# An encoder block at norm2: two steps of the third w_up tile, and splits of the first tile's weights, made earlier

## The chip, the cores and the metric

The kernel runs on one NeuronCore of a Trainium2 chip. A core has five engines that run side by side, each with an instruction stream of its own: TensorE (PE in the profile, its weight loads PEld), VectorE (DVE), ScalarE (ACT), GpSimd (POOL) and SyncE (SP), which here only issues DMAs. They wait for each other by semaphores. The metric is the device time of one execution in microseconds (us).

## The reference

One layer of an encoder on a sequence of 1024 positions with 1024 channels, all in float32. After the token mixers the part that matters here is:

```python
x = x + gate1 * (merged @ w_out[i])                       # the out stage
h2 = rmsnorm(x, g_ffn[i]) * (1 + scale2) + shift2          # norm2
u = depthwise_conv_seq(h2 @ w_up[i], conv_w[i], conv_b[i])  # the up stage
u_val, u_gate = jnp.split(u, 2, axis=-1)
x = x + gate2 * ((jax.nn.gelu(u_gate, approximate=True) * u_val) @ w_down[i])
```

`w_up` has 1024 rows and 5632 columns. The residual `x` is needed for all channels before `rmsnorm` has its scale, so norm2 is a point at which one large product ends and the next can't yet start in full.

## The kernel before, in words

**Precision.** Each float32 operand of a product is split into a high part, rounded to TensorE's fast float32 format, and a low part, the rest. A product is then three matmuls: high by high, high weights by low data, low weights by high data. `split` (L57 and L61) and `operand` (L1135, L1136) make the parts: ScalarE copies the high part, GpSimd or VectorE subtracts to get the low part. One matmul multiplies a 128x128 weight block with 512 columns of data.

**The out stage.** `out_tile(hf, m, ...)` makes one 128-channel tile m of `merged @ w_out` for one half hf of the positions: 24 matmuls (L84 to L86), an update of x on VectorE (L1321), a store of x (L1322), a square for the norm on ScalarE (L1327) and a copy of x scaled by the norm's weights (L1328). The weights of the next tile are loaded (L65) and split (whi by ScalarE, wlo by GpSimd) two buffers ahead. The first half hf = 0 is done for all eight m, then its norm (the sums, a broadcast of the scale by four transposes on PE, L111, and VectorE's multiplication L1352) and its operands B11 and B21 (L1309 on ScalarE, L1310 on VectorE), while PE works on hf = 1.

**The up stage.** The product `h2 @ w_up` is done in 22 tiles, each with two weight tiles (value and gate), by a scheme of Strassen's kind with seven products in place of eight. With `STEPS`, the steps of a tile are named by their weights: "11" and "12" (the weights themselves; their data are B11 and B21, which come from the first half hf = 0 alone), and S2, S1, S3, S4 and "22", whose data T2, T1, T3, B22 and T4 need the second half, and so norm2. Each step is 12 matmuls (L1189 to L1191). The profile's tile names follow: whi and wlo are the parts of "11" and "12", wsh and wsl those of S2 and S1 or of S3 and "22", big those of S4, and x holds B22 and T4 among others.

**A tile's weights.** `a_operands` is a generator with four parts, each run by a `next`: the sums S1, S2 and S3 on GpSimd (L1153 to L1155) and the split of "11" and "12"; the split of S2 and S1 and S4's sum on VectorE (L1162); the split of S3 and "22"; the split of S4. `up_load` fetches a tile's raw weights in two DMAs of 512 KB (L1337), one of value and one of gate rows, into `big` buffers or into `wraw`, of which there are two.

**Around norm2.** Tile 0 is loaded in the out stage, and its sums are made there. Its splits come behind the out stage, as do tile 1's first two parts; the buffers for wsh and wsl (three each) lie in the pool `up`, whose memory is the one that the merged operands held until the last tile of the out stage. `products` makes the steps of a tile as a generator; before the change it yields -1 once within each step, and `advance` runs it to the end of a step. From the last out tile on, PE's order is the written one (`late_mm`): the sums of norm2's squares (L98) with the two halves of tile 0's step "11" between them, the broadcast (L111), tile 1's "11", then "12" of tile 0 and tile 1, and, once T2 is there, the S2 steps of both. VectorE computes, in an order written out by hand (`manual_schedule`), the scaling with the broadcast scale (L1449), T2 (L1452, L1310), T1 (L1458, L1136), T3, B22 and T4; GpSimd makes T4's low parts.

**Order elsewhere.** Outside such hand-written stretches a planner chooses the order of each engine's stream ahead of time, from its own model of durations; a stream is then executed in that order. Tiles of one name in one pool are handed out in the order in which the program asks for them, from the buffers that are free. So a load waits for the tile asked for before it as well as for a free buffer. The loop over t then runs the rest of each tile's steps and, between them, the parts of the next tile's `a_operands`.

Of the kernel before, what the change touches and what calls it, by code (L numbers as in the profile page):

```python
# [19 lines left out]
KT = 8  # L20
FF = 22
# [8 lines left out]
def hybrid_encoder(tc, xT, c, w_ada, small, w_in, p1_bias, p23_bias, na_bias, ln2_mult, ident, w_br, w_out,  # L30
# [1111 lines left out]
    def a_operands(raw, n, work, st, lo_eng=pool, last=False):  # L1142


        a11, a12, a21, a22 = raw[0][:, 0], raw[0][:, 1], raw[1][:, 0], raw[1][:, 1]
        ws = big([128, 2, n, 128])
# [9 lines left out]
        hi, lo = (wpool.tile([128, KT, 128], FR, name=t).rearrange("p (a b) m -> p a b m", a=2)[:, :, :n]  # L1156
                  for t in ("whi", "wlo"))
        pair(raw[0], ("11", "12"), hi, lo, lo_eng)
        yield
        hi, lo = (work(t).tile([128, 2, n, 128], FR, name=t, bufs=3) for t in ("wsh", "wsl"))  # L1160
        pair(ws, ("S2", "S1"), hi, lo)
        dve.tensor_tensor(a12, a12, S2, OP.subtract)  # L1162
        yield
        hi, lo = (work(t).tile([128, 2, n, 128], FR, name=t, bufs=3) for t in ("wsh", "wsl"))
        pair(raw[1], ("S3", "22"), hi, lo)
        yield
        s4 = work("wsl").tile([128, 2, n, 128], FR, name="wsl", bufs=3) if last else big([128, 2, n, 128], FR)
        pair(raw[0][:, 1:2], ("S4",), s4[:, 0:1], s4[:, 1:2])
        yield

    def products(st, n, moving, done, seq=range(7), in_psum=False):

        p, c = {}, {}

        def bank(x_):
            p[x_] = ps.tile([128, 512], FT, name="pj", bufs=6)
            return p[x_]

        def tmp(x_):
            c[x_] = wide()  # L1180
            return c[x_]
        for j in seq:
            a, b = STEPS[j]
            x_ = "abcdacd"[j]
            psum = bank(x_) if j < 4 else p[x_]
            whi, wlo = st[a]
            for k in range(n):
                bhi, blo = moving(b, k)
                pe.matmul(psum, whi[:, k], bhi, start=j < 4 and k == 0, stop=False, skip_group_check=True)  # L1189
                pe.matmul(psum, whi[:, k], blo, start=False, stop=False, skip_group_check=True)  # L1190
                pe.matmul(psum, wlo[:, k], bhi, start=False, stop=k == n - 1, skip_group_check=True)  # L1191
# [163 lines left out]

    m2 = []
    sqa = wide()
    for m in range(KT - 1):
# [6 lines left out]
    sts = [{} for _ in range(FF)]  # L1365
# [8 lines left out]
    late = {n: [] for n in ("B22", "T4")}  # L1374

    with tc.tile_pool(name="up", bufs=2, reuse_waits="tile") as work:
        def conv_in(y, t, hf, src):
            act.activation(y[:, halves[hf]], src, AF.Identity, bias=conv[:, 3, t:t + 1], scale=conv[:, 1, t:t + 1])  # L1378

# [12 lines left out]
        def up_products(t, st, seq=range(7)):  # L1392
            u, ys = [{}, {}], {i: big([128, S]) for i in range(2) if t == FF - 1}

            def done(i, hf, src):
                u[i][hf] = src
                if len(u[i]) == 1 and t < 2:
                    return
                with tc.high_priority(offset=-300 if t == FF - 1 else 0):
                    finish(i, hf)  # L1400

            def finish(i, hf):
                if i not in ys:
                    ys[i] = big([128, S])
                for n in range(2) if t < 2 else (hf,):
                    conv_in(ys[i], t + FF * i, n, u[i][n])
                if len(u[i]) == 2:
                    conv_taps(ys[i], t + FF * i, u[i])
                if len(u[0]) + len(u[1]) == 4:
# [1 line left out]
                    dve.tensor_tensor(ys[0], ys[0], ys[1], OP.mult)  # L1411
                    sp.dma_start(a_scr[t], ys[0])
            return products(st, 4, lambda n, k: late[n][k] if n in late else (ops[n][0][:, k], ops[n][1][:, k]), done,
                            seq)

        raw[1] = up_load(1)
        prep = [a_operands(raw.pop(t), 4, lambda t: work, sts[t], dve) for t in range(2)]
        next(prep[0])
        next(prep[1])
        for _ in range(3):  # L1420
            next(prep[0])
        next(prep[1])
        gens = [up_products(t, sts[t], (0, 4, 1, 2, 3, 5, 6)) for t in range(2)]

        def advance(g):
            for j in g:
# [19 lines left out]
        with tc.manual_schedule(engines={act.engine, dve.engine, pool.engine}):  # L1446
# [45 lines left out]
            for k in range(4):  # L1492
                dve.tensor_tensor(m1[4 + k], m1[4 + k], t2[k], OP.subtract)
                late["T4"].append((half_tile(FR), half_tile(FR)))
                operand(m1[4 + k], *late["T4"][k], pool)
        for g in gens:
            advance(g)
        late_mm.close()
        for t in range(FF):
# [1 line left out]
            if t + 2 < FF:  # L1501
                raw[t + 2] = up_load(t + 2)
            if 0 < t < FF - 1:
                nxt = a_operands(raw.pop(t + 1), 4, lambda t: work, sts[t + 1], last=t + 2 == FF)
                next(nxt)
            elif t == 0:
                nxt = prep[1]
            for j in gens[t] if t < 2 else up_products(t, sts[t]):
# [7 lines left out]
                if t == FF - 1 and j == 3:  # L1516
# [3 lines left out]
                            + [("T3h", 2048, G), ("T3l", 2048, G)])  # L1520
                    for _ in range(3):
                        next(more)
    for p in oppools[::-1]:
        p.release()

# [9 lines left out]
        reserve(work1[n], [(n + e, 2048, G) for e in "hl"])  # L1535
    ends = {}
    sts = [{} for _ in jobs]
    first = a_operands(down_load(*jobs[0]), G, work1.get, sts[0])
# [7 lines left out]
    for n, (g0, q) in enumerate(jobs):  # L1546
        nxt = iter(())
        if n + 1 < len(jobs):
            nxt = a_operands(down_load(*jobs[n + 1]), G, work1.get, sts[n + 1])
        if n < 3:  # L1550
            x3_load(n + 1)
        if n == 2:
# [173 lines left out]
```

## Time and profile before

| | |
|---|---|
| median of three runs (lowest to highest) | 1537.97 us (1537.17 to 1539.8) |
| the profiled execution, its span | 1539.41 us, 1537.3 us |
| PE busy | 1499.0 us, 98% of the span |
| DVE, ACT, POOL busy | 996.0, 770.4, 775.8 us |
| mean granted clock of PE | 0.988 of full speed |
| second half of the out stage | about 816 to 857 us from the span's start |
| norm2's sums, broadcast | 856.17 to 862.98 us |
| first S2 step (T2) | 873.23 us |

The span runs from the first to the last instruction of one execution. In a table of stretches each row has the stretch, its length, the busy time of the engine with the number of its records, the granted clock of PE, the busy share of the DMA engines and what they moved in GB/s. A line of waits has who waited for whom, the total in us, how often and the longest. A line of the chain has start, length and what ran, followed back from the last instruction to what released it. A line of the order of time has start, length, engine, source line, operation, tiles written and read, and in brackets the idle time before it and what ended it; several like operations are merged, their number behind the x.

### The profile page before, as it was taken

How to read it: one execution, taken by the hardware profiler on the slowest of the kernel's cores; microseconds unless marked ns; L12 is line 12 of the kernel's file. 1: busy time of each engine (PE TensorE's matmuls, PEld its weight loads, DVE VectorE, ACT ScalarE, POOL GpSimd, SP SyncE). 2: the span in 40 equal slices, each digit the busy share in tenths (PEclk: the TensorE clock that was granted, in tenths of full speed). 3: DMA queues.
4: the chain of work that ended last, by engine and by line, in shares of the span. 5: the costliest groups of instructions: out<-in, count | busy, mean ns of one | idle time of the engine just before them, and what ended most of it. 6: DMA issues, size and time to landing. Idle time of an engine off the chain costs nothing. (4 is left out here: it accounts for less than half of the span.)

```text
span 1537.3 us, 21792 instructions
## 1 busy us (share of the span) xinstructions
PE 1499.0 (98%) x7740; PEld 1270.1 (83%) x7740; DVE 996.0 (65%) x1892; ACT 770.4 (50%) x1437; POOL 775.8 (50%) x640
## 2 busy tenths in 40 slices
PE   8999999999999999999999899999999998999997
PEld 7988888889798998878888677888888887878787
DVE  6675357575656655645525888876666667786765
ACT  4331566666656566643345454444444447475542
POOL 1021344443335444512267668776777765779721
PEclk8999999999999999999999999999999999999999
DMA  9567333333625456577644112222222224523323
GB/s 352 187 240 258 94 106 81 108 91 104 185 82 153 127 140 171 154 241 232 213 141 154 62 62 96 90 82 83 82 82 85 87 79 162 193 75 124 117 55 110
DMA packets 112436, 205.24 MB, mean 134 GB/s; under 512 B 40484, under 2 KB 53156, under 8 KB 112292
## 3 DMA queue, kind: packets, MB, share of 16 engines
q1 hardware_dynamic: 112056, 203.59, 41.1%
q8 instruction: 61, 1.00, 0.3%
q14 instruction: 47, 0.39, 0.1%
q10 hardware_dynamic: 272, 0.26, 0.1%
HBM read 158.73 MB, written 42.47 MB: 131 GB/s over the span
## 5 line engine op out<-in xcount | busy, mean ns | idle before, releaser
L61 POOL TENSOR_TENSOR wlo<-wraw,whi 128x512 fp32r<-128x512 f32 (+1 forms) x96 | 118.3, 1253 | 172.9 <-ACT whi L57 139.1
L84 PE MATMUL pj<-h,whi 128*128 128x512 f32 x448 | 187.7, 419 | 1.8 <-ACT h L207 1.4
L85 PE MATMUL pj<-h,whi 128*128 128x512 f32 x448 | 177.8, 397 | 1.6 <-DVE h L209 1.6
L86 PE MATMUL pj<-h,wlo 128*128 128x512 f32 x448 | 177.2, 396 | 0.0
L61 POOL TENSOR_TENSOR wsl<-big,wsh 128x512 fp32r<-128x512 f32 (+1 forms) x90 | 123.6, 1395 | 47.7 <-ACT wsh L57 47.7
L639 POOL TENSOR_TENSOR wlo<-wraw,whi 128x512 fp32r<-128x512 f32 x58 | 74.9, 1301 | 117.2 <-ACT whi L638 117.2
L589 DVE TENSOR_TENSOR tl<-T,th 128x512 fp32r<-128x512 f32 (+3 forms) x120 | 77.1, 653 | 72.9 <-ACT th L588 71.4
L1384 DVE SCALAR_TENSOR_TENSOR big<-wc,sm,big 128x256 f32<-128x256 f32 (+1 forms) x132 | 106.9, 859 | 16.1 <-ACT big L1378 15.9
L581 ACT ACTIVATE P<-P,st 128x256 f32<-128x256 f32 x128 | 64.1, 502 | 95.9 <-DVE st L580 95.9
L86 PEld LDWEIGHTS pj<-h,wlo 128*128 128x128 f32 x448 | 85.0, 190 | 18.9
L84 PEld LDWEIGHTS pj<-h,whi 128*128 128x128 f32 x448 | 85.6, 191 | 13.6 <-ACT h L207 1.9
L85 PEld LDWEIGHTS pj<-h,whi 128*128 128x128 f32 x448 | 85.6, 191 | 13.2 <-DVE h L209 3.0
L57 ACT ACTIVATE whi<-wraw 128x1024 fp32r<-128x1024 f32 (+2 forms) x52 | 50.7, 975 | 73.0 <-PE pj L85 27.6
L1384 DVE SCALAR_TENSOR_TENSOR big<-pj,sm,big 128x512 f32<-128x512 f32 x132 | 67.0, 563 | 17.6 <-ACT big L1378 17.6
L61 POOL TENSOR_TENSOR wsl<-wraw,wsh 128x384 fp32r<-128x384 f32 (+1 forms) x46 | 54.4, 1204 | 44.6 <-ACT wsh L57 44.4
L910 POOL TENSOR_SCALAR P<-P,stb 128x288 f32<-128x288 f32 (+1 forms) x32 | 40.2, 1257 | 72.1 <-DVE stb L907 64.7
L588 ACT ACTIVATE th<-T 128x512 fp32r<-128x512 f32 (+3 forms) x120 | 65.6, 566 | 20.3 <-PE T L919 14.0
L1378 ACT ACTIVATE big<-wc,sm 128x512 f32<-128x512 f32 x44 | 35.8, 815 | 69.3 <-DVE wc L1202 42.3
L57 ACT ACTIVATE wsh<-big 128x1024 fp32r<-128x1024 f32 (+1 forms) x45 | 44.7, 998 | 46.2 <-POOL big L1154 32.6
L547 POOL TENSOR_TENSOR vv<-vv 128x512 fp32r<-128x512 f32 (+1 forms) x40 | 42.0, 1069 | 48.5 <-ACT vv L546 48.5
L1410 ACT ACTIVATE big<-big 128x1024 f32<-128x1024 f32 x22 | 23.3, 1060 | 80.0 <-DVE big L1384 80.0
L580 DVE CUSTOM_DVE_ANT_0 P<-S,bias 128x256 f32<-128x256 f32 x128 | 48.9, 419 | 21.3 <-PE S L692 17.1
(395 smaller groups left out, 4799.3 us busy)
## 6 DMA issues: line engine op xcount, KB each, us to landing
wraw<-w_in SPq DMA_DIRECT2D x34, 512.0 KB, 4.2
wada<-w_ada SPq DMA_DIRECT2D x31, 512.0 KB, 7.9
big<-w_up SPq DMA_DIRECT2D x22, 512.0 KB, 5.4
wraw<-w_up SPq DMA_DIRECT2D x22, 512.0 KB, 3.7
as<-big SPq DMA_DIRECT2D x22, 512.0 KB, 3.0
big<-as SPq DMA_DIRECT2D x22, 512.0 KB, 8.0
wraw<-w_down SPq DMA_DIRECT2D x24, 384.0 KB, 3.8
gs<-gs SPq DMA_DIRECT2D x32, 256.0 KB, 2.9
```

The lines of the kernel that those rows point to most:

```text
L57: act.activation(hi, raw, AF.Copy)
L61: lo_eng.tensor_tensor(lo[:, i:i + step], raw[:, i:i + step], f(hi)[:, i:i + step], OP.subtract)
L84: pe.matmul(psum, whi[:, k0 + k], mhi, start=k == 0, stop=False)
L85: pe.matmul(psum, whi[:, k0 + k], mlo, start=False, stop=False)
L86: pe.matmul(psum, wlo[:, k0 + k], mhi, start=False, stop=k == n - 1)
L547: pool.tensor_tensor(lo[:m, cs_], f(lo[:m, cs_]), f(vv[:m, cs_, 0:64]), OP.subtract)
L580: dve.tensor_tensor_reduce(pp, d, bias, -1.0, BIG, OP.add, OP.min, mi)
L581: act.activation(pp, pp, AF.Exp, bias=mi, scale=-1.0, accum_out=li)
L588: act.activation(th[:m, :n], pt[:m, :n], AF.Copy)
L589: dve.tensor_tensor(tl[:m, :n], pt[:m, :n], f(th)[:m, :n], OP.subtract)
L639: pool.tensor_tensor(lo[:, i:i + n], raw[:, i:i + n], f(hi)[:, i:i + n], OP.subtract)
L1384: dve.scalar_tensor_tensor(y[:, dst], src, wt, y[:, dst], OP.mult, OP.add)
```

## The change

Four things are done differently, all around norm2.

- Tile 0's weights are loaded at the start of the second half of the out stage, and its sums, the splits of S2 and S1 and of S3 and "22" are asked for after tiles m = 1, 2 and 4 of it. A new pool `up1` gives them buffers of their own (two for wsh, two for wsl) while the out stage still runs; a third wsh and wsl stays in `up`. Tile 0's split of "11" and "12" and S4's come behind tile m = 6, as the fourth part (`w_at=3`).
- The "11" and "12" rows of tile 2's value weights are loaded once more on their own after m = 5 (two DMAs of 256 KB into `half_tile` buffers) and split there, low parts on GpSimd. Tile 2's later `a_operands` then leaves that split out (`w_at=None`).
- `products` yields -1 after each of its first three groups of three matmuls. Nine matmuls of tile 1's step "11" stand ahead of the broadcast; behind it come the last three, tile 2's "11" and then "12" of tiles 0, 1 and 2. Tile 2's two early results are kept in two new buffers `held`, by one more copy on ScalarE, so that its PSUM bank is freed.
- Tiles 1 and 2 take their sums and S4 parts from new buffers `xb` in place of `big`, and tile 2's convolution, like that of tiles 0 and 1, starts when both halves of a result are there.

The core of the diff:

```diff
+    def a_operands(raw, n, work, st, lo_eng=pool, last=False, w_at=0, spot=None):
+        spot = spot or big
...
+        def outer(at):
+            if w_at == at:
+                hi, lo = (wpool.tile([128, KT, 128], FR, name=t).rearrange("p (a b) m -> p a b m", a=2)[:, :, :n]
+                          for t in ("whi", "wlo"))
+                pair(raw[0], ("11", "12"), hi, lo, lo_eng)
+
+        def s_tiles():
+            pools = [work(t) for t in ("wsh", "wsl")]
+            return [p.tile([128, 2, n, 128], FR, name=t, bufs=b) for (p, b), t in zip(pools, ("wsh", "wsl"))]
+        outer(0)
         yield
+        pair(ws, ("S2", "S1"), *s_tiles())
+        if w_at != 3:
+            dve.tensor_tensor(a12, a12, S2, OP.subtract)
         yield
+        pair(raw[1], ("S3", "22"), *s_tiles())
         yield
+        outer(3)
+        if w_at == 3:
+            dve.tensor_tensor(a12, a12, S2, OP.subtract)
...
-                if k == 1:
+                if k < n - 1:
                     yield -1
...
+            elif j == 4 and hold:
+                act.activation(hold[1], psum, AF.Copy)
+                done(0, 0, hold[1])
...
+    up1 = tc.alloc_tile_pool(name="up1", bufs=2, reuse_waits="tile")
+    reserve(up1, (("wsh", 4096, 2), ("wsl", 4096, 2), ("held", 2048, 2)))
+    s_homes = {n: itertools.cycle([(up1, 2)] * 2 + [None]) for n in ("wsh", "wsl")}
...
+    raw = {0: up_load(0)}
+    prep = [a_operands(raw.pop(0), 4, s_home, sts[0], dve, w_at=3)]
+    held = [up1.tile([128, 512], FT, name="held", bufs=2) for _ in range(2)]
     for m in range(KT - 1):
         m2.append(half_tile())
         out_tile(1, m, sqa, m2[m])
-        if m == 3:
-            raw = {0: up_load(0)}
+        if m in (1, 2, 4):
+            next(prep[0])
+        if m == 5:
+            ahead2 = [half_tile().rearrange("p (b m) -> p b m", b=4) for _ in range(2)]
+            for a, r in enumerate(ahead2):
+                sp.dma_start(r, w_up[2][:, 4 * a:4 * a + 4])
         if m > 3:
             pool.tensor_tensor(m2[m - 4], m2[m], m2[m - 4], OP.subtract)
+    next(prep[0])
+    for n, r in zip(("11", "12"), ahead2):
+        sts[2][n] = [half_tile(FR).rearrange("p (b m) -> p b m", b=4) for _ in range(2)]
+        split(r, *sts[2][n], pool)
...
         add_sums(pcol, sqa, True, False)
         next(gens[0])
+        next(gens[0])
         add_sums(pcol, sq, False, True)
         advance(gens[0])
+        for _ in range(3):
+            next(gens[1])
         bc = bcast(rstd_of(pcol, 4), ps, "pbc")
         advance(gens[1])
-        advance(gens[0])
-        advance(gens[1])
+        advance(gens[2])
+        for g in gens:
+            advance(g)
...
-        for g in gens:
+        for g in gens[:2]:
             advance(g)
```

More of the change, by code (lines that the diff above doesn't have):

```diff
@@ L1140, in hybrid_encoder @@
     names = tuple(b for _, b in STEPS)
-    def a_operands(raw, n, work, st, lo_eng=pool, last=False):
+    def a_operands(raw, n, work, st, lo_eng=pool, last=False, w_at=0, spot=None):
+        spot = spot or big
         a11, a12, a21, a22 = raw[0][:, 0], raw[0][:, 1], raw[1][:, 0], raw[1][:, 1]
-        ws = big([128, 2, n, 128])
+        ws = spot([128, 2, n, 128])
         S2, S1 = ws[:, 0], ws[:, 1]
@@ L1155, in a_operands, with products @@
         pool.tensor_tensor(a21, a11, a21, OP.subtract)
-        hi, lo = (wpool.tile([128, KT, 128], FR, name=t).rearrange("p (a b) m -> p a b m", a=2)[:, :, :n]
-                  for t in ("whi", "wlo"))
-        pair(raw[0], ("11", "12"), hi, lo, lo_eng)
+        def outer(at):
[7 more added lines that the diff above has]
+        outer(0)
         yield
-        hi, lo = (work(t).tile([128, 2, n, 128], FR, name=t, bufs=3) for t in ("wsh", "wsl"))
-        pair(ws, ("S2", "S1"), hi, lo)
-        dve.tensor_tensor(a12, a12, S2, OP.subtract)
+        pair(ws, ("S2", "S1"), *s_tiles())
+        if w_at != 3:
+            dve.tensor_tensor(a12, a12, S2, OP.subtract)
         yield
-        hi, lo = (work(t).tile([128, 2, n, 128], FR, name=t, bufs=3) for t in ("wsh", "wsl"))
-        pair(raw[1], ("S3", "22"), hi, lo)
+        pair(raw[1], ("S3", "22"), *s_tiles())
         yield
-        s4 = work("wsl").tile([128, 2, n, 128], FR, name="wsl", bufs=3) if last else big([128, 2, n, 128], FR)
+        outer(3)
+        if w_at == 3:
+            dve.tensor_tensor(a12, a12, S2, OP.subtract)
+        if last:
+            p, b = work("wsl")
+            s4 = p.tile([128, 2, n, 128], FR, name="wsl", bufs=b)
+        else:
+            s4 = spot([128, 2, n, 128], FR)
         pair(raw[0][:, 1:2], ("S4",), s4[:, 0:1], s4[:, 1:2])
         yield
-    def products(st, n, moving, done, seq=range(7), in_psum=False):
+    def products(st, n, moving, done, seq=range(7), in_psum=False, hold=None):
         p, c = {}, {}
@@ L1376, in hybrid_encoder, with extra @@
     with tc.tile_pool(name="up", bufs=2, reuse_waits="tile") as work:
+        up2.append(work)
+        def extra(shape, dtype=FT):
+            return work.tile(shape, dtype, name="xb", bufs=2)
         def conv_in(y, t, hf, src):
```

30 lines of the change are left out of this document (16 added, 14 removed).

## The prediction

> **What bounds the kernel now.** I read the page's first part first, then the table of stretches around norm2, then PE's waits there, then the chain of waits.
>
> ```profile
> PE 1499.0 (98%) x7740; PEld 1270.1 (83%) x7740; DVE 996.0 (65%) x1892; ACT 770.4 (50%) x1437; POOL 775.8 (50%) x640
> ```
>
> PE is the bound, so only time in which PE waits or runs slowly can be won. The table of stretches for PE (us from:to, length, busy time, records, granted clock, DMA share and rate) shows where that is:
>
> ```profile
> 857.00:863.00 6.00, 4.03 (x23) 1.00 0.12 44
> 863.00:873.23 10.23, 10.23 (x40) 0.83 0.00 0
> 873.23:880.23 7.00, 6.09 (x26) 1.00 0.23 75
> 880.23:891.00 10.77, 8.23 (x21) 0.68 0.01 2
> 891.00:908.33 17.33, 17.33 (x77) 1.00 0.27 91
> 908.33:931.00 22.67, 18.96 (x80) 1.00 0.24 79
> ...
> 1000.00:1290.00 290.00, 290.00 (x1281) 1.00 0.26 90
> ```
>
> The last row is the undisturbed pace: 290.00 / 1281 = 0.226 us a matmul, so a step of 12 matmuls takes 2.72. Two stretches ran at a granted clock of 0.83 and 0.68, and three lose time by waits:
>
> ```profile
> ...
> PE pbc L111 <- DVE rs L105: 2.0, 1, 2.0
> PE pj L1190 <- DVE T1lo L1136: 1.4, 2, 1.2
> ...
> ```
>
> The loss by stretch, as length minus matmuls times 0.226: (a) before the four transposes of norm2's broadcast PE idles 1.97. (b) 863.00 to 873.23 holds 36 matmuls (8.14) and the transposes (about 0.35): 1.7 lost to the clock alone. (c) The T2 steps of tiles 0 and 1 are 24 matmuls (5.42) in 7.00: 1.6. (d) 880.23 to 891.00 starts 20 matmuls (4.52; one of the 21 records began before): 6.2 lost, 2.5 of it idle (10.77 - 8.23), the rest slow clock and restarts. (e) 908.33 to 931.00: 79 matmuls started (17.85): 4.8. Sums: a to d 11.5, with e 16.3. The chain of waits says what paces this place:
>
> ```profile
> ...
> 868.15 1.70 DVE T2lo L1310
> ...
> 876.07 0.75 DVE T2lo L1310
> ...
> 880.06 1.68 DVE T1lo L1136
> ...
> 884.17 0.64 ACT T1hi L1135
> ...
> 891.69 1.07 ACT wsh L57
> ...
> 896.27 5.17 POOL x L1136 x4
> ...
> 911.10 1.28 POOL wlo L61
> ...
> 927.71 2.36 POOL wsl L61 x2
> ...
> ```
>
> Up to 884 it is VectorE making T2 and T1, then PE's T1 step (slow), then GpSimd: wsl, T4's low parts, tile 2's sums, its splits, up to 930. So there are two questions: does PE have other work while VectorE makes T2 and T1, and does GpSimd's chain get earlier too.
>
> **The change part by part.**
>
> *Nine matmuls ahead of the broadcast.* `next(gens[1])` three times puts 9 x 0.226 = 2.04 us of tile 1's step "11" where PE idles 1.97. Its weights are just there: VectorE's split of tile 1's low part ends at 860.6, PE reaches its first use at about 861.3.
>
> ```profile
> 858.33 2.30 DVE L61 TENSOR_TENSOR wlo<-wraw,whi 128x1024 fp32r<-128x1024 f32 x1
> ...
> 860.62 0.39 PE L1191 MATMUL pj<-B11hi,wlo 128*128 128x512 f32 x1
> ...
> 862.65 0.18 DVE L105 RECIPROCAL rs<-rs 128x4 f32<-128x4 f32 x1 [0.27 <-ACT rs L104]
> ...
> 862.98 0.72 PE L111 MATMUL pbc<-idt,rs 128*128 128x128 f32 x4 [1.97 <-DVE rs L105]
> ```
>
> 860.85 + 2.04 = 862.9, and the reciprocal ends at 862.83: the broadcast is not later. Gain (a) 1.97. If the split comes late, PE stands in front of the transposes, its written order, and all of T2 waits.
>
> *No clock drop at 863.* The lower clock begins right behind that idle time. With PE fed I take (b) 1.7 as won; bounds 0 and 1.7. [...] Here 1.97 us of idle preceded a granted 0.83, so the measurement decides.
>
> *Twenty-four matmuls between broadcast and T2.* PE then has 3 + 12 + 36 = 51 matmuls, 11.5 us, before T2, where it had 36. From 863.35 T2 starts at 874.9 (873.23 before). VectorE gave T2's first low part at 869.85 and the fourth at 876.82 (chain above); tile 0's T2 step, from 874.9, needs the fourth at 874.9 + 10 x 0.226 = 877.2. So (c), 1.6, is won, and T2 ends at 880.3 as before, with 5.4 us more work done.
>
> *T1.* PE gets there at 880.3 in both kernels, so (d) goes only if VectorE is earlier. Rows of its slowed operations and of GpSimd beside them:
>
> ```profile
> 861.72 9.28 POOL L61 TENSOR_TENSOR wsl<-big,wsh 128x512 fp32r<-128x512 f32 x6
> ...
> 878.22 2.98 POOL L61 TENSOR_TENSOR wlo<-wraw,whi 128x512 fp32r<-128x512 f32 x2 [4.74 <-ACT whi L57]
> ...
> 868.08 1.78 DVE L1310 SCALAR_TENSOR_TENSOR T2lo<-big,ada,T2hi 128x512 fp32r<-128x512 f32 x1
> ...
> 870.97 0.74 DVE L1310 SCALAR_TENSOR_TENSOR T2lo<-big,ada,T2hi 128x512 fp32r<-128x512 f32 x1
> ...
> 879.98 1.75 DVE L1136 TENSOR_TENSOR T1lo<-big,T1hi 128x512 fp32r<-128x512 f32 x1
> ...
> 882.26 0.68 DVE L1136 TENSOR_TENSOR T1lo<-big,T1hi 128x512 fp32r<-128x512 f32 x1
> ```
>
> The same form takes 1.78 or 0.74, and 1.75 or 0.68: about 1.05 more when GpSimd works beside it. Four of the six wsl (tile 0's) leave this place, and so do the two wlo of tile 2 (878.22). I count three or four slowed VectorE operations less, 3 to 4 us: T1's first part at 878 instead of 881.7, the third at about 882 where PE wants it at 881.9. Left over: about 1.0 of the 6.2, the clock staying up. Bounds: 0 and 6.2 left.
>
> *Tile 0's two S splits in the out stage.* Two ScalarE copies (about 1.05 each) and four GpSimd operations (about 1.3 each), and tile 2's two halves: two 256 KB loads on SP, two ScalarE copies, two GpSimd operations, which replace tile 2's one copy and the two of 878.22. SP also carries w_out and the second w_up tile there; their half tiles come free in the order of the pool behind the m = 5 tile, so they are issued near 847, between the two rows below; at the 3.7 us of a w_up load twice their size they are there by 852, and the halves are wanted at 864.
>
> ```profile
> 846.27 0.32 SPq L1322 DMA_DIRECT2D xs<-x  x1
> 849.56 0.33 SPq L1337 DMA_DIRECT2D wraw<-w_up  x1
> ```
>
> ```profile
> wraw<-w_up SPq DMA_DIRECT2D x22, 512.0 KB, 3.7
> ```
>
> Behind them on SP stands the second of these, whose sums tile 1's T2 wants at 877; two more loads of 256 KB in front of it cost nothing there. GpSimd's room and VectorE's state in that stage (the first row has, behind the length, the busy time and records of PE, PEld, DVE, ACT and POOL):
>
> ```profile
> 816.00:857.00 41.00, 41.00 (x191) 34.10 (x190) 26.71 (x32) 21.82 (x32) 29.12 (x22) 1.00 0.45 135
> ```
>
> ```profile
> 822.09 4.87 DVE L1352 TENSOR_TENSOR big<-big,pbc 128x512 f32<-128x512 f32 x8 [3.56 <-PE pbc L111]
> ...
> 824.76 2.57 POOL L61 TENSOR_TENSOR wlo<-wraw,whi 128x512 fp32r<-128x512 f32 x2 [3.40 <-ACT whi L57]
> 829.58 1.85 POOL L1330 TENSOR_TENSOR wc<-wc 128x512 f32<-128x512 f32 x1 [2.25 <-ACT wc L1327]
> ...
> 838.34 3.00 POOL L61 TENSOR_TENSOR wlo<-wraw,whi 128x512 fp32r<-128x512 f32 x2 [0.20 <-ACT whi L57]
> ...
> 827.54 2.73 DVE L1310 SCALAR_TENSOR_TENSOR B11lo<-big,ada,B11hi 128x512 fp32r<-128x512 f32 x4
> 830.19 5.18 DVE L1310 SCALAR_TENSOR_TENSOR B21lo<-big,ada,B21hi 128x512 fp32r<-128x512 f32 x3
> ...
> 840.30 0.39 PE L86 MATMUL pj<-mhi,wlo 128*128 128x512 f32 x1
> ```
>
> GpSimd idles 3.40 and 2.25, which takes the four operations; L1352 is not slowed (0.61 each) while GpSimd runs, L1310 is (1.73 against 0.68). The tight place is w_out tile 5: its first half of wlo ends at 838.34 + 1.50 = 839.84, PE wants it at 840.30, and it hangs on VectorE's update at 835. Each added GpSimd operation beside L1310 costs that chain 1.04, so PE loses 0 if all lie before 827, 3.7 (4 x 1.04 - 0.46) if none does. The first idle stretch alone takes two; I take 0.5. On ScalarE (21.8 us of the 41.0) the copies stand in front of w_out's whi copies at the same tight place. [...]
>
> *Copies and delays.* `held` adds one ScalarE copy of a PSUM bank, under 1 us, and frees the bank; tile 2's convolution starts once both halves are there. ScalarE is busy for half of the span: 0. Tile 0's pair "11", "12" is made behind its S pairs now, but its buffer comes free with w_out tile 6 in both kernels: 0. The third `yield -1` changes nothing where no one counts the yields. The loads of tile 0 come earlier in the text, on a queue that is not the limit: 0.
>
> *Later, to 931.* Tile 2's 24 matmuls were PE's cover at 908.33 for tile 2's S splits; that cover is spent. Before, PE ran its first 12 from 908.33 and reached tile 2's T2 at 911.05; now it is 10.5 earlier and has 12 more behind it, 911.05 - 10.5 + 2.7 = 903.3. GpSimd's chain starts when tile 0's T1 step frees a wsh buffer (ScalarE's copy of 891.69, now near 880.3 + 2.7 + 1.0 = 884), so it moves by 7 to 8: the second half of tile 3's wlo from 911.10 to 904, the wsl of tile 2 behind it from 912.4 to 905.4. PE then runs tile 3's 24 matmuls (5.4) to about 909 and finds tile 2 ready. So something like the old waits of (e) remains. I leave (e) at 0, bounds 2.5 worse and 4.8 better.
>
> **Sum.** 11.5 - 1.0 - 0.5 = 10.0. The profiled execution took 1539.41 (span 1537.3), 1.4 over the median of the three runs, 1537.97: 1529.4 for its like, 1528 as median.
>
> **The rivals.**
>
> 1. *The T1 wait and its clock drop stay.* If VectorE is not faster (GpSimd's tile 1 splits and sums just move into its place), a to c go, 5.3, and (d) stays with the wsh release; for it speaks that the chain from 863 to 884 is VectorE's own. Tile 2's chain then stays too, PE waits up to 2.5 for tile 3's wlo but saves about that in (e): 1533. Against it: six GpSimd operations fewer. That PE's order is as written is no question, since it is by hand there.
>
> 2. *GpSimd holds the out stage, and the kernel ends slower.* Place: 816 to 857. GpSimd has 29.1 us of 41.0 there; at the contended 1.73 its 22 operations and the 6 new ones are 48 us. PE would lose 7.4 there, the clock falls as at 884 (6.2 - 2.5 = 3.7), and tile 2's halves, last in GpSimd's queue, stop PE once more in its written order in front of T2 (about 3): 14.1 against a gain of 10.5, so 1541.5. At 1.28 uncontended the 28 take 35.8; the gain is gone when they take 44.8, from 20 contended ones on. For it: 0.46 us of margin at 840. Against it: 12 us of GpSimd idle time there, and L1352 not slowed.
>
> 3. *It does not reach the end.* Tile 3's weights come late as well, PE stands at 903 for what it no longer has to cover with: of 10.0, 5.4 of borrowed work and the 2.5 go back: about 1536. For it: the chain is GpSimd's from 892 to 930. Against it: six GpSimd operations (about 9 us) leave that side.
>
> 4. *The drops of the clock are not due to the waits.* Then b (1.7) and the clock's part of d (3.7) stay: 10.0 - 5.4 = 4.6, 1533.4. For it: 908 to 931 lost 4.8 at a granted clock of 1.00. Against it: both slow stretches begin behind idle time. [...]
>
> **How the numbers follow.** Forecast 0.60 (own range 1523.5 to 1532), rival 1 0.12, rival 4 0.04, rival 3 0.12, rival 2 0.12. The bound for a difference is 0.2%, 3.1 us, so same is 1534.9 to 1541.0. Forecast, rival 1 and rival 4 are faster (0.76); rival 3 is same but for 0.01 slower (a wait longer than all it saves), rival 2 slower: same 0.11, slower 0.13. The range: from 1523, which takes most of (e) as won, to 1537, which takes in rivals 1, 3 and 4.
>
> **What would show it.** Right: no wait of PE on rs at the broadcast; a granted clock of 1.00 between 860 and 905; T2 starting about 11.9 behind the broadcast instead of 10.2; T1 waits under 1.5 in all; no PE wait between 816 and 857; tile 1's last step ends near 903. Wrong: a clock below 1 behind a T1 wait (rival 1), a wait on wlo in the out stage (rival 2), a wait over 3 us on wsh or whi between 900 and 910 (rival 3).

## The result, and the profile after

The changed kernel takes 1533.99 us (median of 16 runs, 1528.42 to 1537.12), the kernel before 1538.55 beside it (16 runs, 1536.04 to 1543.0): a ratio of 0.9967, 95% interval 0.9955 to 0.9978. It is faster by 4.6 us, and the forecast was 10.0. The profiled executions took 1535.67 (span 1533.8) and 1539.41 (span 1537.3).

The busy time of PE fell by 4.6 us (of the 5100 matmuls of 128x512 in its trace 24 take over 0.55 us, most of them 0.63, where 44 did before; most of the others take 0.39); the other engines do nearly the same work as before, ScalarE with two instructions more (part 1 of the page of the changed kernel):

```profile
PE 1494.4 (97%) x7740; PEld 1267.5 (83%) x7740; DVE 994.6 (65%) x1892; ACT 771.6 (50%) x1439; POOL 774.2 (50%) x640
```

The stretches of PE that the prediction showed, cut at the same places (us from:to, length, busy time and records of PE, granted clock, DMA share and rate):

```profile
857.00:863.00 6.00, 6.00 (x34) 1.00 0.12 45
863.00:873.23 10.23, 10.23 (x48) 1.00 0.15 51
873.23:880.23 7.00, 7.00 (x33) 1.00 0.01 2
880.23:891.00 10.77, 10.40 (x47) 1.00 0.00 1
891.00:908.33 17.33, 15.65 (x68) 1.00 0.34 113
908.33:931.00 22.67, 16.98 (x64) 0.85 0.32 112
931.00:960.00 29.00, 29.00 (x129) 1.00 0.18 64
```

Up to 891 PE is now fed, at full clock. Behind it there are two stretches that lose more than before: 891 to 908, where the kernel before was busy throughout, and 908 to 931, where the clock drops too, to 0.85. From 931 to 960 nothing is lost.

To add this up, I take for every matmul the distance to the next one's start and count what it has over 0.2267 us (a step of 12 is 2.72), leaving out what is under 0.02. From 850 to 1000 the kernel before loses 17.38 and the changed one 11.98. Split at 892: 11.73 and 5.65 before, 0.93 and 11.05 after. So 10.8 us were won, and 5.4 of it were lost again within 40 us. The up stage, from its first matmul behind the out stage to the first of the down stage, took 437.92 and takes 432.42: 5.5 less, which is the same 5.4. Its length without the loss is 420.5 and 420.4, and in all the kernels below it lies between 420.3 and 420.7, so this loss explains the whole of their differences in this stage. The out stage ends 0.25 earlier (856.98, 856.73); in the kernels below it ends between 854.8 and 860.0, so 0.25 is scatter. The down stage, to the end of the span, is 2.25 longer (242.40, 244.65); in the kernels below it takes 240.3 to 244.7 without following the changes, so I count this as scatter too, whose source was not looked for. 5.50 + 0.25 - 2.25 = 3.5, the difference of the two spans; the medians differ by 4.6.

The matmuls that carry the forecast's times (PE in order of time: start, length, operation, and in brackets the wait ahead of it and what ended it):

```profile
862.64 0.60 PE L111 MATMUL pbc<-idt,rs 128*128 128x128 f32 x4
...
874.68 0.39 PE L1204 MATMUL pj<-T2hi,wsh 128*128 128x512 f32 x1
...
882.24 0.50 PE L1205 MATMUL pj<-T1lo,wsh 128*128 128x512 f32 x1 [0.37 <-DVE T1lo L1136]
...
917.92 0.50 PE L1204 MATMUL pj<-T2hi,wsh 128*128 128x512 f32 x1 [1.27 <-ACT wsh L57]
...
923.02 0.79 PE L1204 MATMUL pj<-x,xb 128*128 128x512 f32 x1 [3.90 <-DVE wc L1214]
```

The broadcast no longer waits, T2 follows it after 12.04 us, and the only wait at T1 is 0.37. Then the waits of PE from 892 to 1000 (total, times, longest):

```profile
PE pj L1204 <- DVE wc L1214: 3.9, 1, 3.9
PE pj L1204 <- ACT wsh L57: 2.4, 2, 1.3
PE pj L1204 <- ACT x L1135: 0.5, 1, 0.5
PE pj L1206 <- POOL wsl L61: 0.5, 1, 0.5
```

The longest is for a PSUM bank: L1214 is VectorE's addition that reads out step S1 of tile 2, and PE's next product, tile 2's S4, adds to that same bank and so has to come behind the reading. The waits on wsh (1.14 and 1.27) and wsl are for ScalarE and GpSimd, 2.9 us together: ScalarE's wsh copies wait for GpSimd's sums. The chain of waits tells why L1214 is late (start, length, what; lines left out are marked):

```profile
889.65 1.79 DVE big L1536
...
892.23 1.19 POOL x L1136
...
898.16 1.25 POOL xb L1154
...
900.82 1.76 DVE wraw L1171
...
905.37 11.70 DVE big L1426 x14
...
918.67 2.29 DVE big L1453
920.97 1.40 DVE big L1426
922.37 0.61 DVE wc L1214
923.02 0.79 PE pj L1204
923.82 0.43 PE pj L1205
```

It runs through T4's sums on VectorE (L1536), T4's low parts on GpSimd (L1136), tile 2's sums (L1154 to L1156), and then through 14 of the taps of the convolutions (L1426), a gelu product (L1453) and the additions among them. Behind the wait the matmuls come 0.43 apart instead of 0.23. So GpSimd's chain, which the prediction followed, hands over to VectorE at 900.8.

### The profile page after: what moved, and what is told of

Same layout as the page of the kernel before. It is cut to its first block, busy times and chain, and to the rows that moved or that the text cites. A ratio compares the mean times of both kernels' runs of the same rounds, so it can differ in the third digit from the quotient of the medians.

```text
span 1533.8 us, 21797 instructions
## 1 busy us (share of the span) xinstructions
PE 1494.4 (97%) x7740; PEld 1267.5 (83%) x7740; DVE 994.6 (65%) x1892; ACT 771.6 (50%) x1439; POOL 774.2 (50%) x640
## 4 chain that ended last, share of the span: by engine, by line
PE 50%; POOL 8%; DVE 7%; ACT 3%; issue 3%; DMA 3%; DVEq 0%; POOLq 0%; ACTq 0%
PE pj L1204 8%; PE pj L1205 8%; PE pj L1206 8%; PE pj L84 6%; PE pj L86 6%; PE pj L85 6%; POOL wsl L61 2%; DMA wraw<-w_down 2%; PE pj L365 2%; PE O L932 2%; POOL wlo L61 2%; DVE big L1426 1%; PE T L919 1%; PE S L897 1%; DVE kl L340 1%
## 5 line engine op out<-in xcount | busy, mean ns | idle before, releaser
L61 POOL TENSOR_TENSOR wsl<-big,wsh 128x512 fp32r<-128x512 f32 (+1 forms) x86 | 116.6, 1376 | 43.4 <-ACT wsh L57 43.4
L1426 DVE SCALAR_TENSOR_TENSOR big<-wc,sm,big 128x256 f32<-128x256 f32 (+1 forms) x129 | 101.0, 827 | 15.1 <-ACT big L1420 15.1
L1426 DVE SCALAR_TENSOR_TENSOR big<-pj,sm,big 128x512 f32<-128x512 f32 (+1 forms) x129 | 66.4, 563 | 15.7 <-ACT big L1420 15.7
L903 ACT ACTIVATE P<-P,stb 128x288 f32<-128x288 f32 (+1 forms) x64 | 36.4, 569 | 50.3 <-DVE stb L901 50.2
L1225 DVE TENSOR_TENSOR pj<-pj,wc 128x512 f32<-128x512 f32 x33 | 22.9, 695 | 53.1 <-PE pj L1206 53.1
```

The source lines that it names most:

```text
L61: lo_eng.tensor_tensor(lo[:, i:i + step], raw[:, i:i + step], f(hi)[:, i:i + step], OP.subtract)
L1426: dve.scalar_tensor_tensor(y[:, dst], src, wt, y[:, dst], OP.mult, OP.add)
```

## The experiments

All but e5 are edits of the changed kernel. "Lost" is the sum above. The times of the kernel before, beside them, were 1538.47 (e1, e2, e4, e5), 1539.54 (e6 to e9), 1539.08 (e10 to e12) and 1540.53 (e13).

```
kernel              time     ratio to before [95%]    lost 850-892  892-1000  up stage
before            1538.55                                 11.73        5.65     437.92
after             1533.99   0.9967 [0.9955, 0.9978]        0.93       11.05     432.42
e1_no_loan        1542.54   1.0025 [1.0013, 1.0038]        7.97       14.01     442.47
e5_nine           1539.83   1.0012 [0.9997, 1.0027]        9.03        9.21     438.70
e2_half_taps      1533.49   0.9968 [0.9956, 0.9981]        0.90       10.41     431.85
e4_taps_behind    1533.39   0.9965 [0.9950, 0.9981]        0.89       11.48     433.01
e6_half_loan      1534.52   0.9967 [0.9954, 0.9981]        0.90       11.37     432.70
e7_pool_light     1527.76   0.9921 [0.9897, 0.9946]        0.90        5.08     426.34
e8_half_taps5     1529.97   0.9942 [0.9923, 0.9961]        0.90        6.83     428.14
e9_both_light     1525.66   0.9904 [0.9871, 0.9936]        0.91        5.25     426.49
e10_raw2_big      1541.09   1.0013 [1.0001, 1.0024]        3.80       15.02     439.19
e11_raw2_taps     1538.34   0.9996 [0.9983, 1.0008]        3.78       14.33     438.62
e12_raw2_t4dve    1540.96   1.0006 [0.9994, 1.0017]        3.78       14.30     438.50
e13_lows_dve      1534.82   0.9965 [0.9955, 0.9976]        0.92       10.78     432.19
```

**Are the terms a to d worth what was forecast, and each by itself?** e1 keeps the early splits and the nine matmuls, but not tile 2's 24 ahead of T2:

```
-        advance(gens[2])
-        for g in gens:
+        for g in gens[:2]:
```

> The changed kernel without tile 2's two steps between the broadcast and T2; they come in their old place. Tile 0's early splits and the nine matmuls stay. Theory V: PE's 24 matmuls only moved, so about 5.4 us of waits come back before T1 ends (VectorE sets T1 in both) and about 5 us go after 900, where the loss is again near 5 instead of 9.9: 2 to 5 us under the kernel before, within 2 of the changed one. Theory G: the loss after 900 stays 8 to 10 and the waits before T1 come back: no faster than the kernel before.

e5 is the kernel before with the nine matmuls ahead of the broadcast and nothing else of the change:

```
-                if k == 1:
+                if k < n - 1:
                     yield -1
...
         next(gens[0])
+        next(gens[0])
...
+        for _ in range(3):
+            next(gens[1])
         bc = bcast(rstd_of(pcol, 4), ps, "pbc")
```

> The kernel before with only the nine matmuls of tile 1 moved ahead of the broadcast (12 matmuls ahead as groups of three). The prediction's terms a and b, taken alone, say 3.7 us under the kernel before. If VectorE's chain from the broadcast to T1 sets when T1 ends, what is won at 861 to 867 is waited out again at T2 and T1: within 1 us of the kernel before.

Neither is faster than the kernel before, and e1 is slower: theory G's outcome. PE's waits at T2 and T1 in e1, then in e5 (rows from PE in order of time):

```profile
872.52 0.50 PE L1205 MATMUL pj<-T2lo,wsh 128*128 128x512 f32 x1 [0.90 <-DVE T2lo L1328]
...
883.90 0.49 PE L1204 MATMUL pj<-T1hi,wsh 128*128 128x512 f32 x1 [0.69 <-ACT T1hi L1135]
```

```profile
870.89 0.51 PE L1190 MATMUL pj<-T2lo,wsh 128*128 128x512 f32 x1 [1.93 <-DVE T2lo L1310]
...
882.37 0.51 PE L1189 MATMUL pj<-T1hi,wsh 128*128 128x512 f32 x1 [1.01 <-ACT T1hi L1135]
```

e1 loses 6.23 at T2 and 1.46 at T1, e5 6.73 and 1.79, the kernel before 1.49 and 6.05: about the same in sum, 7.69, 8.52 and 7.54, only earlier. So the terms were no prices that add up one by one: VectorE gives T2 and T1 at its own times, and (c) and (d) are won only where PE has other work to last until T1. The borrowed 24 matmuls (5.4 us) are that work. What (a) and (b) save is still there at 892, where e1 has lost 3.76 and e5 2.70 less than the kernel before.

Behind 892 both lose more than that again. e1 loses 14.01 there although it borrowed nothing; its longest waits are 3.28 and 3.84 us, ahead of 928.53 and 934.41, both on VectorE (L1426, L1214). So a lead is lost there whether the work was borrowed or not, and it is not shown that the 5.4 us which the changed kernel loses again are the 5.4 us of its 24 matmuls: that the numbers agree may be luck. The early splits, by themselves, shorten nothing.

e6 was to lend only one of the two steps:

```
-        for g in gens:
+        for g in gens[:2]:
             advance(g)
         t2 = big([128, 2, 512])
```

> The changed kernel with only tile 2's first step (12 matmuls, 2.7 us) ahead of T2; its second comes in its old place. The stretch from norm2's first matmul of the up stage to the first of the down stage took 437.9 us before and 432.4 in the changed kernel. If another engine's pace decides what PE keeps of its lead (theory L), the half that is not made early is waited for before T1 ends and not waited for behind 900: 431 to 434. If the lead itself is what counts (theory P, the prediction's sum), half the gain goes: 434 to 436.

It does not tell: tile 2's second step was placed among the T2 matmuls all the same (between 870.64 and 875.40), so it is the changed kernel once more, down to the wait of 3.90 on L1214, and its time agrees.

**Is the new loss the order of one queue?** In e4 VectorE takes tile 1's taps behind the L1214 that PE waits for:

```
+                if t == 1:
+                    waiting.append((finish, i, hf))
+                    return
...
+                if t == 2 and j == 2:
+                    with tc.issue_after(behind[0]):
+                        for fin, i, hf in waiting:
+                            fin(i, hf)
```

> Same work as the changed kernel; only VectorE's order differs: the twelve convolution operations of tile 1 and the product behind them wait for tile 2's two additions (of its S2 and S1 steps). Theory V (VectorE's block of 24 convolution operations of tiles 0 and 1 stands in front of tile 2's addition, PE waits 3.9 us for it, and the clock falls behind that wait, 2.1): the loss of 7.7 us at 916 to 927 shrinks to about 2, and the time is 4 to 6 us under the changed kernel's, 8 to 10 under the kernel before. Theory G (GpSimd's chain of splits paces 900 to 930): PE waits for wsh or wsl by as much as it no longer waits for VectorE, and the time stays 3 to 5 under the kernel before.

The wait at 919 to 923 goes, the loss does not. The waits of PE on VectorE in e4, 856 to 1000:

```profile
PE pj L1206 <- DVE wc L1216: 3.0, 3, 1.7
PE pj L1206 <- DVE held L1233: 2.6, 1, 2.6
PE pj L1206 <- DVE wc L1221: 1.7, 1, 1.7
```

They stand at 931, 937, 941 and 957 instead, and 11.48 is lost in place of 11.05. This order decides where PE waits, not how long. Neither theory held in full: the wait moved as in V, the time stayed near G's, but PE's new waits are on VectorE and not on wsh or wsl.

**Whose work is it?** e2 takes 12 of the taps of tiles 0 and 1 away, e8 half of the taps of tiles 0 to 4:

```
-        def conv_taps(y, t, ph):
+        def conv_taps(y, t, ph, short=False):
...
+            if short:
+                return
...
-                    conv_taps(ys[i], t + FF * i, u[i])
+                    conv_taps(ys[i], t + FF * i, u[i], t < 5)
```

(e2 has `t < 2`.)

> The changed kernel without three of the six convolution operations of each half of tiles 0 and 1 (the taps of the following position are left out there, so the output is not the reference's): twelve VectorE operations of about 0.8 us less, some 10 us. Theory V: the wait of 3.9 us on VectorE and the slow clock behind it go, 4 to 6 us under the changed kernel, 8 to 10 under the kernel before. Theory G: no change against the changed kernel, 3 to 5 under the kernel before.

> The changed kernel without three of the six convolution operations of each half in tiles 0 to 4 (the output is not the reference's): about 5 us of VectorE work less in each tile. Theory L with VectorE's load as the pace: the loss of 10 us behind 898 falls to 2 to 4 and the stretch takes 424 to 427. With GpSimd as the pace: the waits stay, 8 to 10, 430 to 433. With tiles 0 and 1 alone so lightened the loss was 9.7 and the stretch 431.9.

e7 lightens GpSimd: ScalarE copies stand in the place of its subtractions for the low parts of tiles 2 to 5. e9 is e7 and e8 together.

```
+        if lo_eng is act:
+            act.activation(lo, raw, AF.Copy)
+            return
...
+                nxt = a_operands(raw.pop(t + 1), 4, s_home, sts[t + 1], act if t < 5 else pool,
+                                 last=t + 2 == FF, rest=act if t < 5 else pool,
```

> The changed kernel, with the low parts of tiles 2 to 5 made by ScalarE copies of the raw weights in place of GpSimd subtractions (so the low parts, and the output, are not the reference's): some 10 us of GpSimd work less in each of these tiles, 4 us of ScalarE more. Theory L with GpSimd as the pace (its sums end late, VectorE's S4 sum waits for them, and tile after tile the additions behind it in VectorE's queue, on which PE waits): the loss of 10 us behind 898 falls to 2 to 4, the stretch takes 424 to 427, and the time is 10 to 13 under the kernel before. With VectorE as the pace: the loss stays at 8 to 10, 431 to 433, 4 to 6 under the kernel before.

> Both of the two: low parts of tiles 2 to 5 by ScalarE and half of the convolution operations of tiles 0 to 4 left out (the output is not the reference's). If one of the two engines is the pace, this is like the run that lightened that one. If only both together (each slows the other where they work side by side), the loss behind 898 falls to under 3 here, 423 to 426, and stays above 6 in each of the two alone. If it is neither, but the planned order of PE (an addition on VectorE stands between two steps of a tile that PE runs one behind the other), some 6 to 10 us of waits stay here too.

Two tiles' taps (e2) change the loss by 0.6 and leave three waits on L1214, 20 us apart:

```profile
PE pj L1204 <- DVE wc L1214: 6.9, 3, 2.4
```

Five tiles' taps (e8) take 4.2 off it, between the outcomes expected for VectorE and for GpSimd as the pace; GpSimd's low parts (e7) take 6.0 off, with the up stage and the time that were expected for GpSimd as the pace and a loss of 5.1 above the expected 2 to 4; both together (e9) take off no more than e7. In e7 the waits on VectorE behind 900 are gone, although VectorE has all of its own work; what is left, above all one wait of 2.6, is on ScalarE, which e7 itself fills. So e9, which keeps that wait, can't show what lightening both is worth. The stretches of all engines, 20 us each (length; busy time and operations of PE, PEld, DVE, ACT, POOL; granted clock; DMA), first one of the kernel before, then the changed kernel's, then e7's:

```profile
900.00:920.00 20.00, 18.39 (x81) 14.89 (x80) 18.05 (x26) 10.53 (x13) 15.75 (x12) 1.00 0.16 63
```

```profile
880.00:900.00 20.00, 19.10 (x84) 15.19 (x83) 20.00 (x29) 11.07 (x17) 10.99 (x8) 1.00 0.23 79
900.00:920.00 20.00, 16.19 (x68) 12.10 (x66) 19.70 (x24) 13.53 (x16) 18.83 (x14) 1.00 0.18 54
920.00:940.00 20.00, 16.98 (x66) 13.90 (x67) 17.85 (x21) 5.05 (x6) 16.77 (x11) 0.83 0.29 105
```

```profile
900.00:920.00 20.00, 17.41 (x70) 13.94 (x70) 15.74 (x26) 19.63 (x24) 4.70 (x4) 0.91 0.23 80
920.00:940.00 20.00, 20.00 (x89) 16.54 (x89) 15.60 (x23) 12.71 (x17) 9.06 (x6) 1.00 0.37 132
```

In the changed kernel VectorE is busy for 20.00 and 19.70 of 20 us, the latter with 24 operations; in e7 26 operations take it 15.74. In 900 to 920 VectorE waits only once for GpSimd, 0.27 us ahead of 900.82, so PE waits for VectorE's own queue and not for a late result of GpSimd in it. What made VectorE's operations longer stands in VectorE's groups by shape, 900 to 940 (the last numbers before the bar and behind it: count, busy us, mean ns). The changed kernel, then e7, where these lines are numbered three higher:

```profile
L1426 DVE SCALAR_TENSOR_TENSOR big<-wc,sm,big 128x256 f32<-128x256 f32 x4 | 5.6, 1420 | 0.0
...
L1453 DVE TENSOR_TENSOR big<-big 128x1024 f32<-128x1024 f32 x2 | 4.0, 2000 | 0.0
...
L1426 DVE SCALAR_TENSOR_TENSOR big<-pj,sm,big 128x512 f32<-128x512 f32 x3 | 2.2, 740 | 0.0
```

```profile
L1456 DVE TENSOR_TENSOR big<-big 128x1024 f32<-128x1024 f32 x3 | 3.7, 1223 | 0.5 <-ACT big L1455 0.5
...
L1429 DVE SCALAR_TENSOR_TENSOR big<-wc,sm,big 128x256 f32<-128x256 f32 x5 | 3.4, 673 | 0.4 <-ACT big L1423 0.4
...
L1429 DVE SCALAR_TENSOR_TENSOR big<-pj,sm,big 128x512 f32<-128x512 f32 x3 | 2.2, 743 | 0.0
```

Operations with two inputs in SBUF take 1420 ns in the changed kernel, where GpSimd is busy for 35.6 of the 40 us, and 673 in e7, where it is for 13.8; 2000 and 1223; the one whose first input is in PSUM (pj) takes 740 and 743. The changed kernel alone shows the same: from 860 to 1000, VectorE's 128x512 operations on two SBUF inputs take 0.68 to 0.75 us where no GpSimd operation runs beside them (25 of them) and 0.68 to 1.78 where one does (24); those that read PSUM take 0.67 to 0.75 in either case (52). So GpSimd's work costs VectorE time, in these groups up to 1.1 us (1.78 against 0.68) in an operation on two SBUF inputs, and none in those that read PSUM. Through what it does so was not shown.

**Can the load be moved?** Four more kernels keep the whole computation. e10 loads tile 2's raw weights into another buffer, so that their sums can run in the 18.24 us in which GpSimd is idle ahead of 887.59:

```
-            r = big([128, KT, 128]) if t in (0,) or t > 1 and t % 2 else wpool.tile([128, KT, 128], FT, name="wraw")
+            r = big([128, KT, 128]) if t in (0, 2) or t > 1 and t % 2 else wpool.tile([128, KT, 128], FT, name="wraw")
```

> The whole computation, with one difference to the changed kernel: the third tile's raw weights go to a buffer of `big`, so that they needn't wait for the second tile's, and their sums and splits can lie in the 18.24 us in which GpSimd is idle ahead of 887.59. Theory that GpSimd's and VectorE's joint load behind 898 sets the loss: some 3.9 us (the three sums) to 8 us of GpSimd's work leaves the stretch 898 to 931, the loss behind 898 falls from 10.28 to between 5 and 8 us, and the time from about 1534 to 1530 to 1532. Rival, that ScalarE's copies (wsh) or VectorE's own order set it: the sums come early, the loss stays at 9 to 11 us and the time at 1533 to 1535.

Neither expectation came: it is slower by 7 us than the changed kernel. The sums did move to 869.40, but beside them stands VectorE's chain to T2 and T1. VectorE in order of time, the changed kernel, then e10:

```profile
871.68 0.68 DVE L1495 TENSOR_TENSOR wc<-x,big 128x512 f32<-128x512 f32 x1
872.28 0.68 DVE L1515 TENSOR_TENSOR x<-x,x 128x512 f32<-128x512 f32 x1
```

```profile
871.77 1.77 DVE L1495 TENSOR_TENSOR wc<-x,big 128x512 f32<-128x512 f32 x1
873.46 1.78 DVE L1515 TENSOR_TENSOR x<-x,x 128x512 f32<-128x512 f32 x1
```

Two operations of 0.68 take 1.77 and 1.78, T2 and T1 come later, PE loses 3.80 ahead of 892, and T4's low parts on GpSimd start at 897.21 instead of 892.23, also because a wsl of tile 2 (3.45 us) now stands ahead of them. Behind 892, 15.02 is lost although GpSimd is busy for only 13.99 + 15.79 = 29.8 us of 900 to 940, where it was 35.6. So GpSimd's idle time there was the cover of VectorE's chain, and its load behind 898 alone is not what sets the loss. PE's waits behind 892 are 4.5 on L1214, 3.3 on L1426 and 2.7 on T4's high part, where the changed kernel has 3.9, none and 0.5: 2.2 of the 4.0 lost more stand at T4, which comes late here, and the rest was not taken apart.

e11 adds e4's order to e10, and e12 moves T4's four low parts from GpSimd to VectorE:

```
-                operand(m1[4 + k], *late["T4"][k], pool)
+                operand(m1[4 + k], *late["T4"][k], dve)
```

> e10 with e4's order of VectorE (the second tile's taps behind the third tile's first additions). Joint load: the order alone moved the loss without shrinking it (10.75), and with GpSimd lighter it does no more than e10, within 1 us of its time. Rival, that both the order and the load have to be mended for the wait at 919 to 923 to go: 1 to 4 us below e10.

> e10 with T4's four low parts (1.5 us each on GpSimd, 5.93 together) on VectorE instead, at 0.7 to 1.1 us each: 6 us off GpSimd, 3 to 4 us onto VectorE, in 880 to 900, where VectorE is busy throughout. Joint load: the total of both falls by 2 to 3 us, the loss behind 898 by up to that beside e10, time 1 to 3 us below e10. Rival, VectorE alone is the pace: T4's and T3's halves end 3 to 4 us later, the loss rises by as much, time 2 to 4 us above e10.

Both lose within 0.8 of e10 in all. e11's time is 2.8 below e10's; its up stage is only 0.6 shorter, so the rival's 1 to 4 us were met in time but not at this place. e12's expectations both failed: 6 us of work changed its engine and the loss stayed.

e13 makes the low parts of tiles 2 and 3 on VectorE:

```
-                nxt = a_operands(raw.pop(t + 1), 4, s_home, sts[t + 1], last=t + 2 == FF,
+                nxt = a_operands(raw.pop(t + 1), 4, s_home, sts[t + 1], dve if t < 3 else pool,
+                                 last=t + 2 == FF, rest=dve if t < 3 else pool,
```

> The whole computation, with one difference to the changed kernel: the low parts of tiles 2 and 3 (twelve operations of 128x512, which take 1.3 to 1.75 us each on GpSimd between 903 and 940) are made by VectorE, where such an operation takes 0.68 with GpSimd idle beside it. GpSimd loses some 18 us of work behind 903, VectorE gains 8 to 12 and loses what GpSimd's operations add to its own (e7: 3.96 us in 900 to 920, 2.25 in 920 to 940). Theory that GpSimd's work slows VectorE and the sum of both counts: the loss of 892 to 1000 falls from 11.05 to 6 to 9 us, time 1530 to 1532. Rival, VectorE's own work counts most, and adding to it costs its full length: the loss rises to 13 to 17 us, time 1537 to 1540.

It lands between the two expectations, at the changed kernel's own loss (10.78 for 11.05), but not at the same places: PE waits 2.08 us on one of the low parts that VectorE now makes (ahead of 916.51), and 1.51 and 1.41 on VectorE's additions (ahead of 950.29 and 963.19). Its stretches:

```profile
900.00:920.00 20.00, 16.11 (x62) 12.14 (x62) 19.74 (x26) 12.70 (x15) 10.42 (x7) 0.92 0.17 54
920.00:940.00 20.00, 20.00 (x89) 16.56 (x88) 15.25 (x24) 5.66 (x9) 4.89 (x3) 1.00 0.30 105
```

GpSimd's 35.6 us became 15.3, and VectorE is as full in 900 to 920 as it was (19.74): what GpSimd no longer adds to its operations, its new work takes up. From 920 to 940 it is less full (15.25) and PE waits for nothing, and that gain is lost at 950 and 963. Taken together, VectorE is the queue that PE runs into, and GpSimd's work is part of its load; how much of the loss is due to each was not separated. None of the complete kernels beats the changed one beyond its interval.

## Why the prediction was wrong, and where it was right

*(a) to (d), the broadcast, T2, T1 and the clock: right, as a sum.* 11.5 was named, with 1.0 left over, so 10.5; measured 11.73 to 0.93, which is 10.8. T2 was forecast 11.9 behind the broadcast and came 12.04, T1's waits under 1.5 and came to 0.37, the clock 1.00 from 860 to 905, and it is 1.00 up to 908. What the working had wrong is that it priced them one by one: e5 kept 2.70 of (a) and (b) up to 892 and e1 3.76, both had nothing of it in the end, and (c) and (d) did not come at all in e1, without the 24 matmuls.

*The out stage, 0.5 lost: right within its bounds.* There is one wait on wlo of 0.31 at 823.61, where no wait was forecast, and none at the tight place. Summed as above from 816 to 856, the loss is 0.19 before and 0.68 after: 0.49 more. Rival 2, GpSimd holding that stage, fell.

*The clock drops of (b) and (d) go with their waits: right.* From 860 to 908 the clock is 1.00, and 0.83 came back in 920 to 940, behind the wait of 3.90. So rival 4 fell, although its 1533.4, a gain of 4.6, is the measured time: that is luck, since the slow clock that it kept in (b) and (d) is gone. Rival 1 fell with T1's wait.

*"Later, to 931": this step failed.* The term (e) was left at 0, with 2.5 as the worst; what is lost behind 892 grew by 5.4 (5.65 to 11.05). With the measured terms the sum is 10.8 - 0.5 - 5.4 = 4.9, beside the measured 4.6. The step rested on GpSimd's chain moving forward by 7 to 8 us. GpSimd in order of time, before and after (tile 1's wsl, T4's low parts, tile 3's wlo):

```profile
892.83 3.44 POOL L61 TENSOR_TENSOR wsl<-wraw,wsh 128x512 fp32r<-128x512 f32 x2 [11.64 <-ACT wsh L57]
896.22 5.22 POOL L1136 TENSOR_TENSOR x<-big,x 128x512 fp32r<-128x512 f32 x4
...
909.49 2.89 POOL L61 TENSOR_TENSOR wlo<-big,whi 128x512 fp32r<-128x512 f32 x2 [4.17 <-ACT whi L57]
```

```profile
887.59 3.30 POOL L61 TENSOR_TENSOR wsl<-wraw,wsh 128x512 fp32r<-128x512 f32 x2 [18.24 <-ACT wsh L57]
892.23 5.93 POOL L1136 TENSOR_TENSOR x<-big,x 128x512 fp32r<-128x512 f32 x4 [1.35 <-ACT x L1135]
...
912.17 3.19 POOL L61 TENSOR_TENSOR wlo<-big,whi 128x512 fp32r<-128x512 f32 x2
```

The wsl came 5.2 earlier, T4's low parts 4.0, since they wait for VectorE's L1536, and tile 3's wlo, which was to come 7 earlier, 2.7 later. PE was where the prediction had it (tile 1 done near 903), tile 2's splits came 1.14 late, and then there was what the prediction had not looked at: VectorE, at 20.00 of 20 us in 880 to 900 and 19.70 in the next 20, read out a PSUM bank 3.90 us after PE was ready for it, and behind that wait the matmuls ran slow (0.43 us apart instead of 0.23). The prediction took VectorE to matter up to T1, and only GpSimd behind it.

*Rival 3, "it does not reach the end", was half right.* It said that the borrowed 5.4 us go back, and 2.5 more. 11.05 - 5.65 = 5.4 were lost again, and not the 2.5; e1, which loses 14.01 there without borrowing, makes the agreement of the two 5.4 doubtful. Its sign, a wait over 3 us on wsh or whi between 900 and 910, came to 1.14. Its reason, GpSimd's chain alone, was not the one: e13 took 20 us off GpSimd's work from 900 to 940 and the loss in all stayed.

## What to carry to other kernels

Work that an engine does earlier to fill a wait can turn out to be a loan: follow the trace on to where the engine would have done that work, and ask which other engine has to be faster for the lead to last. Read the busy time of all the other engines in that later stretch, not only of the one whose chain is seen now: here VectorE, at 18.05 us of 20 in the kernel before, was the next wait. And idle time of an engine whose work slows the critical one is not free; filling it can cost more than it brings: in e10 two of VectorE's operations took 1.77 and 1.78 us where they had taken 0.68 each, and the time rose by 7 us.

## What the hardware showed that was not expected

In the changed kernel, from 860 to 1000, GpSimd's work stretches VectorE's operations on two SBUF inputs by up to 1.1 us each (from 0.47 to as much as 1.56 us for 128x256, from 0.68 to 1.78 for 128x512), and this is part of what made VectorE the pace of a stage that looked like GpSimd's own.

The granted clock fell behind a wait of 3.90 us (matmuls 0.43 us apart for the next four us, 0.83 granted in 920 to 940), and in the kernel before behind 1.97 (0.43 apart for three us, 0.83 granted in 863 to 873); e4's waits of 2.65, 1.13 and 1.71 us left it at 1.00 in every 20 us from 900 to 960. Waits of nearly one length do both: matmuls 0.43 apart came behind 2.08 in e13 (0.92 granted in 900 to 920), and none behind 2.17, 2.34 and 2.38 in e2 (1.00 in every 20 us from 900 to 960). By these rows neither the length of a wait nor a sum of waits nearby decides alone; what does was not tried.
